# Feed-forward left sides formed during the output projection and parked in DRAM; residual steps tied to later pairs

## The chip, the core and the metric

One core of one Trainium2 chip runs the whole kernel as one program. The metric is device time in microseconds (us), the median over runs; lower is better. The kernel before took 1450.34 us (median of 3 runs, 1446.51 to 1451.52). The engines are named as on the profile page: PE is TensorE (matmuls), DVE is VectorE, ACT is ScalarE, POOL is GpSimd, and SP is SyncE, whose queue issues nearly all DMAs in program order.

## The reference, cut to what matters

The block normalises, projects, mixes attention with gated linear attention, and ends like this (1024 tokens, D = 1024, feed-forward width 4096, float32):

```
x  = layernorm(alpha * x + merged @ w_out)          # output projection, first layer norm: "x1"
ff = square(relu(x @ w_ff1 + b_ff1)) @ w_ff2 + b_ff2
x  = layernorm(alpha * x + ff)
```

## The kernel before, in words

**Precision.** Every float32 operand is split into a rounded high part and a low remainder: ACT casts the high part, DVE subtracts it from the operand for the low part (`split_to`, `halve`). A product is three matmuls per 128 rows of contraction: high by high (line 100), high by low of the moving side (line 101), low by high (line 102). A side is one such split operand of 128 x 512.

**Output projection** (lines 948 to 952 and the loop from 1018). The first 512 columns run in two halves of the contraction for all eight token tiles; the second 512 columns follow tile by tile. After each tile DVE adds the residual (line 930), takes the statistics (936, 941, 942) and normalises (976). PE then transposes the tile (`x1t`, line 997), ACT applies gain and bias (1000), and DVE forms differences of quarters (992), which are split into sides.

**First feed-forward matrix** (`pair1`). Two blocks of 128 hidden columns make a pair; there are 16 pairs. Each pair is a 2 x 2 by 2 x 2 block product done with seven products in place of eight (m1 to m7, each 12 matmuls). The weight's quarters A11, A12, A21, A22 give left sides A11, A12, A22, S1 = A21 + A22, S2 = S1 - A11, S3 = A11 - A21 and S4 = A12 - S2. The activations' quarters B11 to B22 give right sides T1 = B12 - B11, T2 = B22 - T1, T3 and T4. A pair's raw weight is loaded by two DMAs of 512 KB (line 1056); nine DVE operations on 128 x 512 (four sums or differences, five low parts) and five ACT casts make S1 to S4 and A22. A11 and A12 of pairs 0 and 1 are split earlier ("early", line 1029).

**The first two pairs** run side by side with the last transposes (lines 1194 to 1226): m1 and m2 of both, then m5, m3, m6, m7, m4. m5 needs T1, which needs the transposes of the last token tile.

**Residual.** x1 waits in DRAM (`x1dr`). For the second layer norm, sixteen pieces of 128 x 512 are loaded, multiplied by the gain (line 1247), given a bias (1248) and written back. The source hangs two of them on each of pairs 2 to 9; three broadcast vectors of 512 KB (line 1233) come first.

**What sets the order.** The source states the work; a scheduler with its own cost model then lays down each engine's instruction order at build time. At run time each engine, and SP's queue, goes through its list strictly in order. `issue_after` keeps the scheduler from putting an instruction ahead of a named one on the same engine; it adds no wait at run time. Sides live in a ring of seven buffers (`fraw`, `fwhi`, `fwlo`, `wc`), raw weights in a ring of five.

## Time and profile before

| what | value |
|---|---|
| median of 3 runs | 1450.34 us |
| the profiled execution | 1448.67 us, span 1446.9 us |
| PE busy | 1400.9 us, 97% of the span |
| DVE busy | 994.1 us, 69% |
| ACT busy | 622.4 us, 43% |
| DMA, mean | 158 GB/s, 227.98 MB in all |
| stretch 813.7 to 910.0 | 96.3 us, of which PE is busy 83.5, DVE 84.4 |

Times of rows are counted from the span's start. The stretch in the last line is where the first pairs of the feed-forward begin: it starts at the end of the products of "early". Before and after it PE is busy without a break.

### The profile page before, as it was taken

The numbers are of one execution on the slowest core, as the hardware profiler recorded it, in microseconds if no ns is written. First come the engines' busy times: TensorE is split into PE (matmuls) and PEld (weight loads), VectorE is DVE, ScalarE is ACT, GpSimd is POOL, SyncE is SP. The second block draws the span as 40 slices with busy tenths as digits, with TensorE's granted clock in tenths as the row PEclk, the third lists the DMA queues.
The fourth block names the chain that finished last, engine by engine and source line by source line (L and its number), as shares of the span: only waits on it lengthen the run. The fifth ranks groups of instructions, "written<-read, shape, count | busy, mean of one in ns | idle before, by whom it ended". The sixth has DMA issues, their size and how long they took to land.

```text
span 1446.9 us, 18910 instructions
## 1 busy us (share of the span) xinstructions
PE 1400.9 (97%) x6842; PEld 1167.8 (81%) x6842; DVE 994.1 (69%) x1710; ACT 622.4 (43%) x1180; POOL 84.6 (6%) x67
## 2 busy tenths in 40 slices
PE   8999889989999999999999898999999999999997
PEld 6989887877888888878888676888888888888885
DVE  5155745777555578566646988776666798786988
ACT  5244532434433344345405743555455633433333
POOL 2220312000000000022000000000000000000001
PEclk9999999999999999999999899999999999999999
DMA  7242403495543454275612476854433883544313
GB/s 232 70 132 63 153 31 123 153 280 180 178 144 128 137 165 136 82 231 167 242 58 87 146 243 240 302 170 154 156 139 116 287 331 117 189 131 145 100 47 117
DMA packets 122522, 227.98 MB, mean 158 GB/s; under 512 B 20685, under 2 KB 53709, under 8 KB 122428
## 3 DMA queue, kind: packets, MB, share of 16 engines
q1 hardware_dynamic: 122284, 226.57, 47.4%
q8 instruction: 54, 0.88, 0.3%
q14 instruction: 40, 0.33, 0.1%
q10 hardware_dynamic: 144, 0.20, 0.0%
HBM read 155.32 MB, written 72.44 MB: 157 GB/s over the span
## 4 chain that ended last, share of the span: by engine, by line
PE 86%; DVE 6%; DMA 5%; issue 1%; ACT 1%; SPq 0%; POOL 0%; DVEq 0%; ACTq 0%; POOLq 0%
PE ps L100 16%; PE ps L102 16%; PE ps L101 16%; PE mm L100 10%; PE mm L101 10%; PE mm L102 10%; PE avp L733 3%; DMA x1dr<-res 2%; PE sc L699 2%; PE tr L720 1%; DMA res<-x1dr 1%; PE sc L372 1%; DMA tb<-in_b_ff 1%; DVE T L982 0%; DVE xr L992 0%
## 5 line engine op out<-in xcount | busy, mean ns | idle before, releaser
L93 POOL TENSOR_TENSOR wlo<-raw,whi 128x768 fp32r<-128x768 f32 (+2 forms) x26 | 57.4, 2212 | 505.0 <-ACT whi L91 497.6
L981 ACT CAST T<-hp 128x1024 fp32r<-128x1024 f32 x36 | 37.9, 1052 | 110.0 <-PE ps L101 70.3
L100 PE MATMUL mm<-whi,x 128*128 128x272 f32 (+1 forms) x256 | 81.0, 317 | 0.0
L101 PE MATMUL mm<-wlo,x 128*128 128x272 f32 (+1 forms) x256 | 80.6, 315 | 0.0
L102 PE MATMUL mm<-whi,x 128*128 128x272 f32 (+1 forms) x256 | 80.5, 314 | 0.0
L101 PE MATMUL ps<-B,B 128*128 128x512 f32 x160 | 62.4, 390 | 0.0
L102 PE MATMUL ps<-B,B 128*128 128x512 f32 x160 | 62.3, 389 | 0.0
L100 PE MATMUL ps<-B,B 128*128 128x512 f32 x160 | 61.0, 391 | 0.5 <-ACT B L981 0.5
L100 PE MATMUL ps<-T,fraw 128*128 128x512 f32 x128 | 52.2, 409 | 7.6 <-ACT T L981 5.3
L102 PE MATMUL ps<-B,T 128*128 128x512 f32 x144 | 56.2, 390 | 0.0
L100 PE MATMUL ps<-B,T 128*128 128x512 f32 x144 | 56.2, 390 | 0.0
L102 PE MATMUL ps<-T,T 128*128 128x512 f32 x144 | 56.1, 390 | 0.0
L101 PE MATMUL ps<-T,T 128*128 128x512 f32 x144 | 56.0, 389 | 0.0
L100 PE MATMUL ps<-T,T 128*128 128x512 f32 x144 | 56.0, 389 | 0.0
L101 PE MATMUL ps<-B,T 128*128 128x512 f32 x144 | 56.0, 389 | 0.0
L1360 DVE TENSOR_TENSOR acc<-ps,acc 128x512 f32<-128x512 f32 x68 | 45.8, 689 | 12.9 <-PE ps L102 12.2
L982 DVE TENSOR_TENSOR T<-hp,T 128x1024 fp32r<-128x1024 f32 x36 | 44.0, 1223 | 15.3 <-ACT T L981 15.2
L100 PE MATMUL mm<-x,whi 128*128 128x512 f32 x120 | 47.6, 408 | 6.9 <-ACT x L146 5.8
L709 ACT ACTIVATE e<-e,sm 128x256 f32<-128x256 f32 (+2 forms) x96 | 43.2, 452 | 24.5 <-DVE sm L704 24.4
L101 PE MATMUL ps<-T,fraw 128*128 128x512 f32 x128 | 52.0, 406 | 1.2 <-DVE T L982 1.2
L102 PE MATMUL ps<-T,fraw 128*128 128x512 f32 x128 | 51.5, 404 | 0.0
L542 DVE TENSOR_TENSOR cr<-cu,mm 128x512 f32<-128x512 f32 x42 | 33.7, 805 | 23.2 <-PE mm L102 22.3
(424 smaller groups left out, 4166.5 us busy)
## 6 DMA issues: line engine op xcount, KB each, us to landing
hdr<-c SPq DMA_DIRECT2D x112, 256.0 KB, 2.5
hp<-hdr SPq DMA_DIRECT2D x56, 512.0 KB, 3.7
spill<-cr SPq DMA_DIRECT2D x56, 256.0 KB, 2.6
gate<-spill SPq DMA_DIRECT2D x32, 256.0 KB, 3.0
wa<-in_w SPq DMA_DIRECT2D x16, 512.0 KB, 5.0
wb<-in_w SPq DMA_DIRECT2D x16, 512.0 KB, 6.8
praw<-in_wfm SPq DMA_DIRECT2D x14, 512.0 KB, 4.2
pwhi<-in_wfm SPq DMA_DIRECT2D x14, 512.0 KB, 3.8
```

The costliest lines, as they stand in the source:

```text
L93: (lo_eng or G).tensor_tensor(lo, raw, hi.bitcast(F32), op=OP.subtract)
L100: T.matmul(ps, lh, rh, start=first and i == 0, stop=False, skip_group_check=more)
L101: T.matmul(ps, lh, rl, start=False, stop=False, skip_group_check=more)
L102: T.matmul(ps, ll, rh, start=False, stop=last and i == n - 1, skip_group_check=more)
L372: T.matmul(ap[d][:, i], kd[pr, cs], qd[pr, cs], start=True, stop=True)
L542: V.tensor_tensor(o, a, b, op=OP.add)
L699: T.matmul(sps[i][:, pr, 0:w], q[ps_, pr], k[ps_, pr, 0:w], start=True, stop=True)
L709: issued["exp"] = A.activation(e, e, AF.Exp, bias=sm[:, h:h + 1], scale=-1.0, accum_out=sm[:, 4 + h:5 + h])
L733: T.matmul(av[:, h * 64:h * 64 + 64], b["et"][h % 2][p0:p0 + vv.shape[0], h // 2, j], vv[:, h * 64:h * 64 + 64], start=j == 0, stop=j == n ...
L981: A.copy(o[:, 0], src)
L982: V.tensor_tensor(o[:, 1], src, o[:, 0].bitcast(F32), op=OP.subtract)
L1360: V.tensor_tensor(m, p, m, op=OP.add)
```

## The change

The pairs 0 and 1 no longer load their raw weight there and no longer form S1 to S4 and A22 there. A function `park` does this during the first half of the output projection, interleaved with its matmul calls: load, nine DVE operations and five casts for each pair, and each finished side (high and low, 512 KB) is written to a DRAM tile `sdr`. In the first pairs, `parked` then loads each side back into its ring buffer by one DMA. The raw loads of pairs 2 and 3 are issued a little earlier in the source. The residual's vectors and pieces move from pairs 2 to 9 to pairs 4 to 11, and are bound by `issue_after` to the latest raw weight load (loads) and to the add of m6 of their pair (arithmetic); the switch of the side memory to the second matrix moves from pair 12 to pair 13.

```diff
--- before.py
+++ after.py
@@ -107,6 +107,7 @@
...
     ygdr = dr.tile([4, 128, S], F32, name="ygdr")
+    sdr = dr.tile([2, 5, 128, 2, 512], F32, name="sdr")
     yadr = dr.tile([2, 128, S], F32, name="yadr")
...
@@ -946,9 +947,48 @@

     w += [wo_piece(wob, k2) for k2 in (2, 3)]
     ps = [bank8() for _ in range(8)]
-    for ks in (range(0, 4), range(4, 8)):
-        for t in range(8):
-            wout(t, 0, w, ps[t], ks)
+
+
+
+    sp_ = P.open("sides", reuse_waits="tile")
+    s_raw, s_out = ring(sp_, [128, 2, 512], F32, 2, "sraw"), ring(sp_, [128, 2, 512], F32R, 2, "sout")
+    s_sum = sp_.tile([128, 512], F32, name="ssum")
+
+    def park(j):
+        wr = {}
+
+        def keep(n, src):
+            o = s_out()
+            halve(o[:, 0], o[:, 1], src)
+            SP.dma_start(sdr[j, n], o.bitcast(F32))
+
+        def load():
+            for f in range(2):
+                t = s_raw()
+                SP.dma_start(t, io["w1"][2 * j + f].rearrange("p (h k) f -> p h (k f)", h=2))
+                wr[f] = t
+
+        def s1():
+            V.tensor_tensor(s_sum, wr[1][:, 0], wr[1][:, 1], op=OP.add)
+            keep(0, s_sum)
+
+        def s2():
+            V.tensor_tensor(s_sum, s_sum, wr[0][:, 0], op=OP.subtract)
+            keep(1, s_sum)
+
+        def s4():
+            V.tensor_tensor(s_sum, wr[0][:, 1], s_sum, op=OP.subtract)
+            keep(2, s_sum)
+
+        def s3():
+            V.tensor_tensor(wr[1][:, 0], wr[0][:, 0], wr[1][:, 0], op=OP.subtract)
+            keep(3, wr[1][:, 0])
+
+        return [load, s1, s2, s4, s3, lambda: keep(4, wr[1][:, 1])]
+
+    merge_streams([lambda t=t, ks=ks: wout(t, 0, w, ps[t], ks) for ks in (range(0, 4), range(4, 8)) for t in range(8)],
+                  park(0) + park(1))
+    P.close("sides")
     w = [load_w(io["wo"][1, k2], [128, 2, 512], V) for k2 in range(4)]
     P.close("wob")
     P.close("woa")
@@ -1053,7 +1093,7 @@
                 st["w"] = {}
                 for f in range(2):
                     w = f1_raw().bitcast(F32)
-                    SP.dma_start(w, io["w1"][2 * j + f].rearrange("p (h k) f -> p h (k f)", h=2))
+                    issued["load"] = SP.dma_start(w, io["w1"][2 * j + f].rearrange("p (h k) f -> p h (k f)", h=2))
                     for h in range(2):
                         st["w"][f, h] = w[:, h]
             return st["w"]
@@ -1064,22 +1104,34 @@
             c[nm] = cs[(7 * j + n if j > 1 else 4 * j + n if n < 4 else 4 + 3 * j + n) % 10]
             return c[nm]

+        def parked(nm, n):
+            st[nm] = o = f1_side().bitcast(F32R)
+            SP.dma_start(o.bitcast(F32), sdr[j, n])
+
         def s1():
+            if j < 2:
+                return parked("S1", 0)
             w = raw()
             st["s"] = f1_sum()
             V.tensor_tensor(st["s"], w[1, 0], w[1, 1], op=OP.add)
             st["S1"] = left(st["s"])

         def s3():
+            if j < 2:
+                return parked("S3", 3)
             w = raw()
             V.tensor_tensor(w[1, 0], w[0, 0], w[1, 0], op=OP.subtract)
             st["S3"] = left(w[1, 0])

         def s2():
+            if j < 2:
+                return parked("S2", 1)
             V.tensor_tensor(st["s"], st["s"], raw()[0, 0], op=OP.subtract)
             st["S2"] = left(st["s"])

         def s4():
+            if j < 2:
+                return parked("S4", 2)
             V.tensor_tensor(st["s"], raw()[0, 1], st["s"], op=OP.subtract)
             st["S4"] = left(st["s"])

@@ -1101,6 +1153,8 @@
             st["A12"] = early(1) if j < 2 else left(raw()[0, 1])

         def a22():
+            if j < 2:
+                return parked("A22", 4)
             st["A22"] = left(raw()[1, 1])

         def m1():
@@ -1117,7 +1171,7 @@

         def m6():
             mm("Y", st["S2"], "T2")
-            V.tensor_tensor(c["u2"], c["u2"], ps["Y"], op=OP.add)
+            issued["add"] = V.tensor_tensor(c["u2"], c["u2"], ps["Y"], op=OP.add)

         def m7():
             mm("W", st["S3"], "T3")
@@ -1183,8 +1237,6 @@
-    p0["raw"]()
-    p1["raw"]()
     SP.dma_start(x1dr[7], acc[7])
     def both(*names):
         for n in names:
@@ -1216,36 +1268,43 @@
     both("m5", "s2", "s4", "m3e")
     sums()
     both("s3")
+    pairs[2]["raw"]()
+    pairs[3]["raw"]()
     xsum("T2", x7, "x7", XR[1][:, 4:8])
     both("m6")
     xsum("T3", xp, "act", XR[1][:, 0:4])
     both("m7", "u3", "c22", "a22")
     xsum("T4", bp, "actb", XR[0][:, 4:8])
-    pairs[2]["raw"]()
-    pairs[3]["raw"]()
     both("h12", "m4", "h21")
     P.close("xraw")


-    resp = P.open("res", side="right", reuse_waits="tile")
-    ga, bb, tb = (resp.tile([128, D], F32, name=n) for n in ("ga", "bb", "tb"))
-    for n, v in (("ln1_g", ga), ("ln1_b", bb), ("b_ff2", tb)):
-        bvec(None, io[n], n, v)
-    V.tensor_scalar(ga, ga, ALPHA, None, op0=OP.mult)
-    V.scalar_tensor_tensor(bb, bb, ALPHA, tb, op0=OP.mult, op1=OP.add)
-    res_t = ring(resp, [128, 512], F32, 4, "res")
+    rs = {}
+
+    def res_open():
+        resp = P.open("res", side="right", reuse_waits="tile")
+        ga, bb, tb = (resp.tile([128, D], F32, name=n) for n in ("ga", "bb", "tb"))
+        with tc.issue_after(issued["load"].ins):
+            for n, v in (("ln1_g", ga), ("ln1_b", bb), ("b_ff2", tb)):
+                bvec(None, io[n], n, v)
+        V.tensor_scalar(ga, ga, ALPHA, None, op0=OP.mult)
+        V.scalar_tensor_tensor(bb, bb, ALPHA, tb, op0=OP.mult, op1=OP.add)
+        rs.update(t=ring(resp, [128, 512], F32, 4, "res"), ga=ga, bb=bb)

     def residual(i):
         t, h = i // 2, slice(i % 2 * 512, i % 2 * 512 + 512)
         r = {}

         def load():
-            r["t"] = res_t()
-            SP.dma_start(r["t"], x1dr[t, :, h])
+            r["t"] = rs["t"]()
+            with tc.issue_after(issued["load"].ins):
+                SP.dma_start(r["t"], x1dr[t, :, h])

         def do():
-            V.tensor_tensor(r["t"], r["t"], ga[:, h], op=OP.mult)
-            V.tensor_tensor(r["t"], r["t"], bb[:, h], op=OP.add)
+
+            with tc.issue_after(issued["add"].ins):
+                V.tensor_tensor(r["t"], r["t"], rs["ga"][:, h], op=OP.mult)
+                V.tensor_tensor(r["t"], r["t"], rs["bb"][:, h], op=OP.add)
             SP.dma_start(x1dr[t, :, h], r["t"])
         return load, [do]

@@ -1282,10 +1341,12 @@
     for j in range(2, NJ):
         st = list(pairs[j]["steps"])
         for i in (2, 5):
-            if j < 10:
-                load, do = residual(2 * j - 4 + (i > 2))
+            if 4 <= j < 12:
+                load, do = residual(2 * j - 8 + (i > 2))
                 st[i] = (lambda a=st[i][0], b=load: (a(), b())), st[i][1] + do
-        if j == 12:
+        if j == 3:
+            st[0] = st[0][0], [res_open] + st[0][1]
+        if j == 13:
             st[0] = st[0][0], [switch] + st[0][1]
         steps += st
     run(steps, 3)
```

The instruction lists show three places. In the changed kernel the lines shown have later numbers: 976 becomes 1016, 982 becomes 1022, 992 becomes 1032.

DVE, from the statistics of the last token tile (acc7) on, before. `xr0` and `xr1` are the transposed quarters; line 1070 is the sum of S1 and line 1075 the difference of S3, for pairs 0 and 1:

```order
L936 BN_STATS sts_6311<-acc7_5685 128x6
L1070 TENSOR_TENSOR c0_5928<-fwlo_6346 128x512
L941 BN_AGGR mv_6314<-sts_6311 128x2
L992 TENSOR_TENSOR xr0_5932<-xr1_5933,xr0_5932 128x4x128
L1075 TENSOR_TENSOR fwlo_6346<-fwlo_6345,fwlo_6346 128x512
L942 TENSOR_SCALAR mv_6314<-mv_6314 128x1
L992 TENSOR_TENSOR xr1_5933<-xr1_5933 128x4x128
L982 TENSOR_TENSOR B22_6263<-xr1_5933,B22_6263 128x4x128
L976 TENSOR_SCALAR acc7_5685<-acc7_5685,mv_6314 128x1024
L1070 TENSOR_TENSOR c0_5928<-fwhi_6342 128x512
L992 TENSOR_TENSOR xr1_5933<-xr1_5933,xr0_5932 128x4x128
L992 TENSOR_TENSOR xr0_5932<-xr1_5933,xr0_5932 128x4x128
```

The same place in the changed kernel:

```order
L937 BN_STATS sts_6363<-acc7_5686 128x6
L942 BN_AGGR mv_6366<-sts_6363 128x2
L943 TENSOR_SCALAR mv_6366<-mv_6366 128x1
L1032 TENSOR_TENSOR xr0_5984<-xr1_5985,xr0_5984 128x4x128
L1016 TENSOR_SCALAR acc7_5686<-acc7_5686,mv_6366 128x1024
L1032 TENSOR_TENSOR xr1_5985<-xr1_5985 128x4x128
L1022 TENSOR_TENSOR B22_6315<-xr1_5985,B22_6315 128x4x128
L1032 TENSOR_TENSOR xr1_5985<-xr1_5985,xr0_5984 128x4x128
L1032 TENSOR_TENSOR xr0_5984<-xr0_5984,xr1_5985 128x4x128
L1032 TENSOR_TENSOR xr0_5984<-xr1_5985,xr0_5984 128x4x128
L1032 TENSOR_TENSOR xr1_5985<-xr1_5985 128x4x128
L1022 TENSOR_TENSOR T1_6439<-xr0_5984,T1_6439 128x384 x4
```

The three operations of pairs 0 and 1 are gone from these rows, and the first pieces of T1 (line 1022, `T1`), which stood 18 rows behind the statistics, stand 11 behind them. On PE, the eight transposes of acc7 stand 12 matmuls earlier than before; the rest of PE's list up to there is the same.

DVE during the first half of the output projection, before: the last parts of the first half's weight (`wo`), the low parts of the second half's weight (`wlo`), then the first evacuation (line 930):

```order
L147 TENSOR_TENSOR wo12_5690<-raw_5687,wo02_5689 128x1024
L147 TENSOR_TENSOR wo13_5696<-raw_5693,wo03_5695 128x1024
L93 TENSOR_TENSOR wlo_5903<-raw_5899,whi_5901 128x1024
L93 TENSOR_TENSOR wlo_5909<-raw_5905,whi_5907 128x1024
L93 TENSOR_TENSOR wlo_5915<-raw_5911,whi_5913 128x1024
L93 TENSOR_TENSOR wlo_5921<-raw_5917,whi_5919 128x1024
L930 SCALAR_TENSOR_TENSOR acc0_5671<-acc0_5671,ps0_5118 128x512
L936 BN_STATS sts_5961<-acc0_5671 128x6
```

The same place in the changed kernel; `sraw`, `ssum` and `sout` belong to `park` of pair 0:

```order
L148 TENSOR_TENSOR wo12_5691<-raw_5688,wo02_5690 128x1024
L148 TENSOR_TENSOR wo13_5697<-raw_5694,wo03_5696 128x1024
L972 TENSOR_TENSOR ssum_5707<-sraw1_5704 128x512
L984 TENSOR_TENSOR sraw1_5704<-sraw0_5703,sraw1_5704 128x512
L148 TENSOR_TENSOR sout0_5705<-ssum_5707,sout0_5705 128x512
L976 TENSOR_TENSOR ssum_5707<-ssum_5707,sraw0_5703 128x512
L93 TENSOR_TENSOR wlo_5955<-raw_5951,whi_5953 128x1024
L93 TENSOR_TENSOR wlo_5961<-raw_5957,whi_5959 128x1024
L148 TENSOR_TENSOR sout1_5706<-ssum_5707,sout1_5706 128x512
L980 TENSOR_TENSOR ssum_5707<-sraw0_5703,ssum_5707 128x512
L148 TENSOR_TENSOR sout0_5705<-ssum_5707,sout0_5705 128x512
L93 TENSOR_TENSOR wlo_5967<-raw_5963,whi_5965 128x1024
```

Pair 0's operations stand before and between the `wlo` parts; pair 1's stand further down, between the evacuations.

SP's queue, where the residual's vectors and first pieces are loaded, before:

```order
L919 DMA ga_6711<-in_ln1_g 128x1024
L919 DMA bb_6712<-in_ln1_b 128x1024
L1056 DMA fwhi_6342<-in_w1 128x1024
L919 DMA tb_6713<-in_b_ff2 128x1024
L1244 DMA res0_6719<-x1dr_87 128x512
L1244 DMA res1_6720<-x1dr_87 128x512
L1244 DMA res2_6721<-x1dr_87 128x512
L1244 DMA res3_6722<-x1dr_87 128x512
L1056 DMA fwlo_6346<-in_w1 128x1024
L1056 DMA w14_6463<-in_w1 128x1024
L1249 DMA x1dr_87<-res0_6719 128x512
```

In the changed kernel, the second two residual loads and the first writes that follow them:

```order
L1301 DMA res2_6893<-x1dr_88 128x512
L1301 DMA res3_6894<-x1dr_88 128x512
L1144 DMA hdr_87<-c0_5980 128x512
L1144 DMA hdr_87<-c9_6516 128x512
L1144 DMA hdr_87<-c5_6512 128x512
L1144 DMA hdr_87<-c0_5980 128x512
L1144 DMA hdr_87<-c6_6513 128x512
L1308 DMA x1dr_88<-res0_6891 128x512
L1308 DMA x1dr_88<-res1_6892 128x512
```

Before, the residual stands directly behind the raw loads of the first pairs, and a piece's buffer is reloaded as soon as it is written. Now two pieces are loaded per pair, and the loads of one pair stand ahead of the writes of the pair before it.

## Rows read from the trace of the kernel before

**Rows 1.** Busy time by stretch: engine busy (x instructions), clock, DMA share, GB/s
```profile
696.00:752.00 56.00, 56.00 (x246) 45.78 (x245) 31.47 (x43) 13.87 (x19) 0.00 (x0) 1.00 0.45 158
813.70:846.00 32.30, 25.74 (x97) 19.79 (x96) 28.84 (x48) 17.91 (x35) 0.00 (x0) 0.84 0.46 162
846.00:866.00 20.00, 19.02 (x82) 15.34 (x83) 18.30 (x31) 10.67 (x18) 0.00 (x0) 1.00 0.65 217
866.00:880.00 14.00, 10.41 (x38) 7.82 (x37) 13.17 (x23) 5.42 (x9) 0.00 (x0) 0.88 0.78 277
880.00:910.00 30.00, 28.32 (x123) 22.68 (x123) 24.08 (x40) 12.06 (x22) 0.00 (x0) 1.00 0.74 252
910.00:950.00 40.00, 40.00 (x176) 32.60 (x175) 28.35 (x46) 22.05 (x38) 0.00 (x0) 1.00 0.74 265
1200.00:1300.00 100.00, 99.50 (x438) 81.90 (x438) 81.49 (x90) 35.16 (x36) 0.00 (x0) 1.00 0.49 153
```

**Rows 2.** Who TensorE waited for, 800 to 960: us in total, times, longest
```profile
PE ps L100 <- DVE c L1126: 1.8, 1, 1.8
PE ps L100 <- ACT fwlo L981: 1.8, 1, 1.8
```

**Rows 3.** Timeline of TensorE: start, duration, [idle before <- releaser]
```profile
803.57 1.04 PE L997 MATMUL ps<-ident,acc 128*128 128x128 f32 x8
...
810.03 1.04 PE L997 MATMUL ps<-ident,acc 128*128 128x128 f32 x8
...
813.47 0.40 PE L102 MATMUL ps<-B,early 128*128 128x512 f32 x1
819.16 1.22 PE L100 MATMUL ps<-T,fraw 128*128 128x512 f32 x2 [5.30 <-ACT T L981]
...
822.18 0.79 PE L101 MATMUL ps<-T,fraw 128*128 128x512 f32 x1 [1.18 <-DVE T L982]
...
826.61 0.53 PE L102 MATMUL ps<-T,fraw 128*128 128x512 f32 x1
...
850.00 0.47 PE L100 MATMUL ps<-B,fwhi 128*128 128x512 f32 x1 [0.58 <-DVE c L1147]
```

**Rows 4.** Timeline of VectorE, 800 to 822
```profile
800.97 0.69 DVE L936 BATCH_NORM_STATS2 sts<-acc 128x6 f32<-128x512 f32 x1
803.65 0.69 DVE L1070 TENSOR_TENSOR c<-fwlo 128x512 f32<-128x512 f32 x1 [1.99 <-DMA fwlo<-in_w]
...
806.80 0.81 DVE L976 TENSOR_SCALAR acc<-acc,mv 128x1024 f32<-128x1024 f32 x1
...
811.13 1.29 DVE L982 TENSOR_TENSOR fraw<-c,fraw 128x512 fp32r<-128x512 f32 x2
...
821.43 0.70 DVE L982 TENSOR_TENSOR T<-xr,T 128x512 fp32r<-128x512 f32 x1
```

**Rows 5.** Timeline of ScalarE, 808 to 819
```profile
808.24 1.15 ACT L981 CAST fraw<-c 128x512 fp32r<-128x512 f32 x2 [0.86 <-DVE c L1070]
...
810.29 1.77 ACT L981 CAST T<-xr 128x384 fp32r<-128x384 f32 x4
...
812.53 2.90 ACT L1000 ACTIVATE xr<-ps,cols 128x128 f32<-128x128 f32 x8
...
818.43 0.68 ACT L981 CAST T<-xr 128x512 fp32r<-128x512 f32 x1
```

**Rows 6.** Line 1247: duration ns min/median/max, first and last start
```profile
L1247 DVE TENSOR_TENSOR res<-res,ga x16: 685/693/700, 845.0 to 898.2; 128x512 f32<-128x512 f32 x16
```

**Rows 7.** Who VectorE waited for, 842 to 906
```profile
DVE res L1247 <- DMA res<-x1dr: 8.4, 9, 2.2
```

**Rows 8.** DMA issues, 690 to 910: count, KB each, median us to landing
```profile
fwlo<-in_w SPq DMA_DIRECT2D x6, 512.0 KB, 5.0
```

**Rows 9.** The low parts wlo, 700 to 760: duration ns, first and last start
```profile
L101 PE MATMUL ps<-wlo,mg x13: 395/396/397, 751.5 to 759.9; 128*128 128x512 f32 x13
...
L93 DVE TENSOR_TENSOR wlo<-raw,whi x4: 1225/1226/1227, 722.4 to 730.9; 128x1024 fp32r<-128x1024 f32 x4
```

## The prediction

> **What bounds the kernel now.** I read the page first: PE is busy 97% of the span, so only stretches where PE idles, or runs at half clock, can give time back. The second view is busy time by stretch [rows 1] (columns after the stretch: its length, then PE, weight loads, DVE, ACT, POOL). From 910 to 950 PE is never idle and does 176 matmuls in 40 us, 0.2273 us each. I use that as the full rate and ask of each stretch what its matmuls would need:
>
> - 813.7 to 846: 97 matmuls need 22.05 of 32.3 us; lost 10.25 (idle 6.56, the rest at a granted clock of 0.84).
> - 846 to 866: 82 need 18.64 of 20; lost 1.36.
> - 866 to 880: 38 need 8.64 of 14; lost 5.36 (clock 0.88).
> - 880 to 910: 123 need 27.96 of 30; lost 2.04.
>
> Together 19.0 us. That is the most this change can win, since PE loses next to nothing before and after.
>
> Third, why. The timeline of PE [rows 3] shows the first loss: after the last product of "early" (813.47) PE idles until 819.16 for the ACT cast of the last piece of T1, then until 822.18 for DVE's low part of it. The 11 matmuls from 822.18 to 826.61 come every 0.44 us instead of 0.23: PE is at the lower of its two levels (1.2 GHz) after the long idle. The timeline of DVE [rows 4] shows what T1 waited behind. The statistics of token tile 7 end at 801.66; then DVE stands 1.99 us for a raw weight of pair 0, and until T1's low part ends at 822.13 it does 12 operations of pairs 0 and 1 (the four sums and differences S1 and S3, the two S2, five low parts, and S4 of pair 0), 0.60 us each when back to back (two in 1.29). ACT has five casts of the same sides in between [rows 5]. The later losses are mainly two waits of 1.8 us for DVE and ACT [rows 2], in a stretch where DVE is busy 94% (866 to 880) and holds the residual: 16 pieces from 845.0 to about 903 [rows 6], two operations each, 32 x 0.60 = 19.2 us, with another 8.4 us of standing for residual loads [rows 7].
>
> **Part 1: S1 to S4 and A22 of pairs 0 and 1 are loaded ready.** Removed from DVE between 803 and about 842: 18 operations x 0.60 = 10.8 us, and the 1.99 us of standing; from ACT ten casts of about 0.52 (two in 1.15, [rows 5]). What is late next? I follow T1 in the changed order. Tile 7's transposes stand 12 matmuls earlier on PE: 810.03 - 12 x 0.233 = 807.2 [rows 3], done at 808.0. DVE is ready for that: without the raw wait and two operations between 801.66 and 806.80, tile 7 is normalised by about 804.4. ACT then sets the pace [rows 5]: tile 6's evacuation of 2.90 us from 804.6, when its transposes end (803.57 + 1.04), a copy to 808.0, T1's four casts of 1.77 to 809.8, one more cast to 810.3, tile 7's evacuation of 2.90 to 813.2, a relu to 813.8, the last cast of T1 to 814.4 (before: 819.1; copy and relu are taken like a cast, 0.5 to 0.6). DVE's low part follows by 815.1 (before: 822.13). So of the 6.56 us idle at the head, about 1.0 us stays, in two gaps of 0.7 and 0.3.
>
> Does the clock fall at these gaps? A wait of 0.58 us before 850.00 [rows 3] lies in a stretch granted 1.00; the waits of 1.8 and 1.8 lie in one granted 0.88 [rows 1, 2]. The new gaps are nearest to the first, so I take no loss; the other end is the 11 slow matmuls of before, 11 x 0.21 = 2.3 us. The Trainium skill ("TensorE: Matmul & The Clock Gate", Part 1: The HAM clock gate) says that half rate is the default and that only recent activity releases the full clock. By that rule any new pause is a risk, and with the clock lost at the head the sum would be 2.3 us worse; the 0.58 us row speaks against it for so short a pause.
>
> After the head PE has m5, m3, m6 and m7 of both pairs, 96 matmuls, 21.8 us without a break if their sides are there. T2, T3 and T4 need twelve more DVE pieces, 7.2 us, so DVE is done by about 825, when m6 begins. The sides come by DMA. The ring buffers of S2 and S4 come free with the last matmuls of the output projection, at about 799.9; their four loads are first in SP's queue there, then x1 and four raw loads of pairs 2 and 3. At 5.0 us to landing [rows 8], and eight transfers of 0.5 MB at the 252 GB/s of the 880 to 910 row, the fourth lands by 808 and the eighth by 817; m3 needs S4 at 815. S3 and A22 reuse buffers that m5 and m6 free at 818 to 828, and are needed from 831. Cost taken: 0. The upper bound is one late load, 5.0 us.
>
> **Part 2: the same work during the output projection.** Added to 707 to 752: 18 DVE operations (10.8 us), ten casts (5.2 us), four loads and ten writes of 0.5 MB. From 696 to 752 DVE is busy 31.5 of 56 us and ACT 13.9 [rows 1], so there is room for both. The order matters more: pair 0's operations stand ahead of the low parts of the second weight half, which were done at 732.1 and which PE first uses at 751.5 [rows 9]. On DVE seven operations, 4.2 us, stand before or between them; on SP the raw loads of that half stand behind one write of a side. Even two loads and a write in series (15 us at 5.0 each) stay within the 19 us of slack. Cost 0. Pair 1's operations stand between evacuations of banks that PE takes up again only 20 us later, so a DVE that stands 5 us for its reload costs nothing either.
>
> **Part 3: the residual.** It leaves the stretch 843 to 903 and comes back as four DVE operations, 2.4 us, in each of pairs 4 to 11. A pair is 84 matmuls, 19.1 us. DVE was busy 71% of 910 to 950, and 2.4 of 19.1 adds 13%: 84%. The nearest row is 1200 to 1300, DVE 81% busy, where PE does 438 matmuls in 100 us and loses 0.45 us. Over eight pairs, 153 us, that is 0.7 us. The other end is what 846 to 910 lost with the same 32 operations in it: 1.36 + 5.36 + 2.04 = 8.8 us. I take the first, because DVE no longer stands for loads: in SP's new order the loads of one pair go out ahead of the writes of the pair before, and before they went out behind the write that freed the buffer. The vectors (line 1233) can still hold DVE once around pair 4; for this and for small waits like the one of 0.58 at 850.00 I put 1.0 us, an estimate.
>
> **Sum.** -19.0 + 1.0 + 0.7 + 1.0 = -16.3 us, against the profiled execution's 1448.67: 1432.4. The median of before is 1.67 above that execution, so the median forecast is 1434.
>
> **Rivals.**
> A. The residual costs the same wherever it stands. DVE runs in order, so four more operations behind m6's add hold up the next evacuation and the next side. For it: the waits of 1.8 us [rows 2]. Against: eight pairs instead of three. Then 8.8 stays: -19.0 + 1.0 + 8.8 + 1.0 = -8.2, 1442; with the clock also lost at the head, 1444.5.
> B. The parked sides arrive late. 14 transfers of 0.5 MB are added to one queue, and S3 and A22 wait there behind stores. For it: 5.0 us per load. Against: the slack above. Each product that waits costs up to 5.0 and some half clock: with two, 1444.
> C. The change doesn't do what it says: T1 was only the first of several waits. ACT sits a step behind DVE, and m6 and m7 wait for T2 and T3 instead, with the residual again in the way in pairs 4 and 5. Gain under 4 us: 1448.
> D. Slower. Every pair from 4 to 11 meets a wait and half clock, as 866 to 880 did (5.36 us). The place is m7's evacuation behind the two residual multiplications. Eight times 5.36 is 43 us against the 17 won: 1476. It decides from 2.1 us per pair. For it: DVE stood for residual loads nine times, up to 2.2 us [rows 7]. Against: the loads now go out a pair ahead.
>
> **How the numbers follow.** Forecast 0.58 (1430 to 1438), A 0.20, B 0.07, C 0.09, D 0.06. About 0.3%, 4.4 us, is what a measurement of this kernel can tell from no change. Forecast, A and B end below 1446: faster 0.85; C is the same, 0.09; slower 0.06. The range 1429 to 1446 takes in all 19 us won at one end, and A with the clock lost and a late load at the other.
>
> **What would show it.** T1's low part ends at about 815 and PE starts the bulk of m5 within 2 us of the end of "early", with the clock at 1.00 from 813 to 846; 97 matmuls of that stretch take 23 to 24 us; the stretch that followed, to pair 4, has no PE wait over 1 us; 696 to 800 has none either, with DVE about 11 us busier; and residual operations lie from about 860 to 1030, two loads a pair, without PE waits beside them. The prediction is wrong if PE waits for `sdr` loads, if the second weight half is late at 752, or if PE loses over 2 us per pair in pairs 4 to 11.

## The result and the profile after

The changed kernel took 1435.28 us (median of 4 runs, 1432.0 to 1435.46) against 1448.65 for the kernel before on the same chip (four runs, of which the 1450.34 at the head is the median of the first three): a ratio of 0.990, 95% interval 0.988 to 0.992. The forecast was 1434. The profiled execution took 1435.09 us (before: 1448.67), so 13.6 us less, where the sum had said 16.3.

The busy time by stretch comes first, engine by engine as in [rows 1]. Three stretches of 32, 64 and 140 us are counted from the end of the last product that reads "early", because everything behind that point starts from it. Before:

```profile
813.87:845.87 32.00, 25.53 (x96) 19.79 (x96) 28.54 (x48) 17.61 (x35) 0.00 (x0) 0.84 0.47 163
845.87:909.87 64.00, 57.68 (x240) 45.75 (x240) 55.54 (x92) 28.14 (x48) 0.00 (x0) 0.97 0.72 246
909.87:1049.87 140.00, 140.00 (x612) 114.55 (x611) 97.22 (x154) 74.32 (x122) 0.00 (x0) 1.00 0.54 189
```

and after, in the same view, with the stretch of the parked work first:

```profile
696.00:752.00 56.00, 56.00 (x246) 45.86 (x245) 38.00 (x54) 20.06 (x29) 0.00 (x0) 1.00 0.72 261
816.94:848.94 32.00, 31.73 (x138) 25.82 (x139) 23.94 (x39) 18.08 (x33) 0.00 (x0) 1.00 0.39 134
848.94:912.94 64.00, 64.00 (x281) 52.43 (x280) 46.50 (x74) 32.38 (x54) 0.00 (x0) 1.00 0.61 206
912.94:1052.94 140.00, 139.06 (x604) 112.75 (x604) 109.22 (x176) 69.33 (x116) 0.00 (x0) 1.00 0.62 223
```

Read the number behind PE's busy time, the matmuls done. At the full rate of about 0.228 us each, the first 32 us win 42 matmuls (9.6 us), the next 64 us win 41 (9.3), and the 140 us in which the residual now stands lose 8 (1.8). The list of PE's waits from 690 to 1110 us is now short (columns as in [rows 2]; u3, line 1180, is the add behind m7); the waits of 5.3, 1.8 and 1.8 of before are gone:

```profile
PE ps L100 <- DVE c L1180: 0.9, 3, 0.5
PE ps L100 <- ACT T L1021: 0.3, 1, 0.3
```

The timelines at the head answer to [rows 3 to 5]. The last product of "early" starts at 816.54; ACT ends its last cast of T1 0.6 us later, and DVE's low part (817.19) follows at once. TensorE:

```profile
816.54 0.40 PE L102 MATMUL ps<-B,early 128*128 128x512 f32 x1
817.21 0.73 PE L100 MATMUL ps<-T,fraw 128*128 128x512 f32 x2 [0.27 <-ACT T L1021]
```

ScalarE and VectorE:

```profile
813.17 2.90 ACT L1040 ACTIVATE xr<-ps,cols 128x128 f32<-128x128 f32 x8
815.92 0.73 ACT L1140 ACTIVATE c<-ps,cols 128x512 f32<-128x512 f32 x1
816.49 0.66 ACT L1021 CAST T<-xr 128x512 fp32r<-128x512 f32 x1
```
```profile
817.19 0.69 DVE L1022 TENSOR_TENSOR T<-xr,T 128x512 fp32r<-128x512 f32 x1 [0.40 <-ACT T L1021]
```

**Where the missing 3 us are.** "early" ends at 816.94 after and at 813.87 before, 3.07 us later, although up to the output projection the instructions stand in the same order on every engine. From that point to the end of the span it is 616.36 us after and 633.03 before: 16.7 us less, against 16.3 forecast. Matched one by one in order, the same matmul starts 0.62 us later after than before from 20 to 120 us, 2.16 us later at 140 and 3.07 us later from 650 on. All of the delay stands ahead of the first load of parked work (711.9), so the moved work did not cause it. Half of it arises between 120 and 140 us. From 115 to 130, before and after:

```profile
115.00:130.00 15.00, 13.83 (x95) 12.51 (x94) 6.68 (x11) 9.11 (x26) 2.44 (x4) 1.00 0.25 67
```
```profile
115.00:130.00 15.00, 13.83 (x85) 12.51 (x84) 5.00 (x9) 9.22 (x26) 2.44 (x4) 0.89 0.25 67
```

PE is idle for the same 1.17 us, yet in one execution the granted clock stays at 1.00 and in the other it falls to 0.89, which costs ten matmuls in this stretch. Of the 12 profiled executions of this study six show 1.00 (94 or 95 matmuls) and six 0.89 (85). A cast on ACT that comes right behind starts at 148.9 to 149.7 in the first six and at 150.5 to 151.4 in the others. The changed kernel's profile fell on one side and before's on the other. The other half of the delay comes in small steps that were not followed up. So below each kernel's time from the end of "early" to the end of its span is given beside its median: it leaves this difference out.

### The profile page after: what moved, and what is told of

It reads as the page before. It is cut to its first block, busy times and chain, and to the rows that moved or that the text cites. A ratio compares the mean times of both kernels' runs of the same rounds, so it can differ in the third digit from the quotient of the medians.

```text
span 1433.3 us, 18978 instructions
## 1 busy us (share of the span) xinstructions
PE 1398.6 (98%) x6842; PEld 1167.5 (81%) x6842; DVE 995.3 (69%) x1710; ACT 621.1 (43%) x1180; POOL 84.5 (6%) x67
## 4 chain that ended last, share of the span: by engine, by line
PE 85%; DVE 7%; DMA 4%; ACT 2%; issue 2%; SPq 0%; POOL 0%; DVEq 0%; ACTq 0%; POOLq 0%
PE ps L100 15%; PE ps L101 15%; PE ps L102 15%; PE mm L100 10%; PE mm L101 10%; PE mm L102 10%; PE avp L734 3%; PE sc L700 2%; PE tr L721 1%; DMA fwhi<-in_w 1%; DMA w<-in_w 1%; PE sc L373 1%; PE av L383 0%; DMA xr<-in_xT 0%; PE sc L344 0%
## 5 line engine op out<-in xcount | busy, mean ns | idle before, releaser
L1140 ACT ACTIVATE c<-c,cols 128x512 f32<-128x512 f32 x48 | 34.7, 725 | 47.9 <-DVE c L1186 32.4
L100 PE MATMUL ps<-T,fraw 128*128 128x512 f32 x128 | 50.6, 397 | 1.2 <-DVE c L1180 0.9
L101 PE MATMUL ps<-T,fraw 128*128 128x512 f32 x128 | 50.1, 392 | 0.0
```

The costliest lines, as they stand in the source:

```text
L100: T.matmul(ps, lh, rh, start=first and i == 0, stop=False, skip_group_check=more)
L101: T.matmul(ps, lh, rl, start=False, stop=False, skip_group_check=more)
L1140: A.activation(q, src, AF.Relu, bias=cols[:, 2 * j + f:2 * j + f + 1])
```

## The experiments

Each kernel ran on one chip beside the kernel before. "From early" is the time in the profiled execution from the end of the last product of "early" to the end of the span; the last column has the matmuls done in the 32, the next 64 and the next 140 us.

| kernel | median us | before, same chip | ratio, 95% interval | from early | matmuls 32 / 64 / 140 |
|---|---|---|---|---|---|
| before | 1448.65 | | | 633.0 | 96 / 240 / 612 |
| the change | 1435.28 | 1448.65 | 0.990 (0.988 to 0.992) | 616.4 | 138 / 281 / 604 |
| the change again | 1430.38 | 1449.21 | 0.987 (0.986 to 0.989) | 615.2 | 138 / 281 / 608 |
| sides only | 1444.83 | 1450.45 | 0.996 (0.995 to 0.997) | 627.8 | 130 / 230 / 612 |
| residual only | 1441.16 | 1450.45 | 0.993 (0.992 to 0.994) | 623.4 | 97 / 280 / 613 |
| tied, pairs 2 to 9 | 1433.17 | 1450.45 | 0.988 (0.987 to 0.990) | 616.9 | 138 / 280 / 603 |
| no residual arithmetic | 1431.06 | 1450.45 | 0.986 (0.985 to 0.988) | 614.2 | 139 / 281 / 613 |
| residual arithmetic twice | 1430.48 | 1450.47 | 0.986 (0.984 to 0.987) | 614.4 | 139 / 281 / 612 |
| parked work twice | 1452.88 | 1450.47 | 1.002 (1.001 to 1.003) | 615.4 | 139 / 281 / 607 |
| order only | 1437.21 | 1450.47 | 0.990 (0.989 to 0.992) | 620.9 | 108 / 280 / 613 |
| tied behind u3 | 1430.14 | 1450.47 | 0.986 (0.984 to 0.988) | 614.3 | 138 / 281 / 613 |
| pair 0 parked, u3 | 1438.33 | 1449.21 | 0.992 (0.991 to 0.993) | 620.4 | 113 / 279 / 612 |

**1. The sides alone.** The residual goes back to pairs 2 to 9, opened ahead of the loop, without ties:

```diff
-            with tc.issue_after(issued["load"].ins):
-                SP.dma_start(r["t"], x1dr[t, :, h])
+            SP.dma_start(r["t"], x1dr[t, :, h])
...
-            if 4 <= j < 12:
-                load, do = residual(2 * j - 8 + (i > 2))
+            if j < 10:
+                load, do = residual(2 * j - 4 + (i > 2))
```

(the same for the multiplications and the vectors).

> The left sides of pairs 0 and 1 are parked as in the changed kernel; the residual stands in pairs 2 to 9 as before, without the two ties. In the order of instructions its 32 operations on DVE then lie in one cluster, right behind the splits of T4. Theory (head and residual are two separate losses): the head is as in the changed kernel (loss after the end of 'early' about 1 us), and about 8.8 us of waits and half clock stay beside the residual; time 1448.7 - 10.25 + 1 = about 1439 to 1440, and PE waits of 1 to 3 us for DVE and ACT within 40 us of the first residual operation. Rival 1 (the residual hurt only because DVE was already late from the sides): PE does not wait beside the residual either, time 1435 as with the whole change. Rival 2 (the residual was the main thing): 1446.

It won 5.2 us from "early" on, less than the 9.3 expected, and no rival fits. For T1 PE waits only 0.3 us, as in the full change. But the cluster of residual operations now starts 20 us behind the end of "early" (833.0) instead of 31 [rows 6] and costs more than it did before: 130 matmuls in 32 us, where the full change has 138, and 230 in 64 us, where before had 240. Busy time by stretch, and two of PE's waits:

```profile
812.90:844.90 32.00, 30.42 (x130) 24.27 (x131) 24.85 (x40) 14.20 (x26) 0.00 (x0) 1.00 0.59 200
844.90:908.90 64.00, 55.00 (x230) 43.48 (x229) 50.71 (x84) 27.93 (x47) 0.00 (x0) 0.95 0.83 291
```
```profile
PE ps L100 <- ACT c L1140: 6.5, 1, 6.5
PE ps L100 <- ACT c L1164: 1.6, 1, 1.6
```

ACT, which PE waits for, itself stands behind DVE, and DVE is never idle there for long: from 850 to 869 its residual operations stand between the steps of the products. So the two parts are not independent. With the residual left where it was, 11.6 us (51 matmuls) are lost behind the head, and the sides' gain is partly eaten. The ties alone decide where the residual stands: built with the residual in pairs 4 to 11 but without the ties, the program has the same instructions in the same order as this kernel, on every engine. The place in the source moved nothing.

**2. The residual alone.** Before, with the residual and its ties as in the change.

> The kernel before with the residual alone moved and tied to pairs 4 to 11; all left sides are formed at the head as before. Theory: the head keeps its loss of about 10 us (PE idle 5 to 6 us for T1, granted clock near 0.84 in the 30 us behind it), and the stretch behind it loses 1 to 2 us instead of 8.8; time 1448.7 - 8.8 + 1.7 = about 1441 to 1442. Rival (the waits behind the head come from the sides' delay, and the residual only fills gaps): the waits stay, time 1447. With the sides alone and this run the two gains should add up to the gain of the whole change, about 13 to 16 us.

It won 9.6 us from "early" on (expected: 7 to 8). Stretches and the whole list of PE's waits from "early" to 1060:

```profile
815.99:847.99 32.00, 25.19 (x97) 19.85 (x98) 29.06 (x49) 18.59 (x37) 0.00 (x0) 0.84 0.27 83
847.99:911.99 64.00, 64.00 (x280) 52.33 (x280) 49.78 (x80) 35.99 (x59) 0.00 (x0) 1.00 0.61 214
911.99:1051.99 140.00, 140.00 (x613) 114.64 (x612) 108.01 (x173) 73.15 (x117) 0.00 (x0) 1.00 0.62 219
```
```profile
PE ps L100 <- ACT T L981: 5.6, 1, 5.6
PE ps L101 <- DVE T L982: 1.2, 1, 1.2
```

The head keeps its whole loss, and the 64 us behind it lose nothing at all: the waits there came from the residual, not from the delayed sides. The rival (1447) is out. The two gains add up to 14.9 us, against 16.7 and 17.8 for two executions of the whole change.

**3. Two pairs earlier.** The ties kept, the residual in pairs 2 to 9.

> The changed kernel with the residual in pairs 2 to 9 instead of 4 to 11, its ties kept (each load behind the raw loads of its pair, each multiplication behind the add of m6). Theory A (the tie, that is four operations per pair instead of a cluster, is what saves): time within 1.5 us of the changed kernel, 1435 to 1437. Theory B (pairs 2 and 3 stand beside the tail of pairs 0 and 1, where DVE has no room): PE waits of over 1 us in pairs 2 and 3, about half of the 8.8 us comes back, 1439.

Theory A holds: 616.9 from "early", within 0.6 us of the change. Its loss sits in one wait of 1.9 us for the add u3, at 980 us, in neither pair 2 nor pair 3.

**4. Without the residual's arithmetic.** The two multiply and add operations are left out, so the residual lacks its scale and bias.

> The changed kernel with the two operations per piece of the residual left out (32 on DVE; the loads and the write-backs stay), so that its output lacks the scale and bias of the first LayerNorm in the residual. Theory: in pairs 4 to 11 the residual costs PE 0.7 us, so the time falls by 0.5 to 1 us, to about 1434.5, which is inside the noise. Rival A (the residual costs the same wherever it stands, 8.8 us): 1427.

From "early" it is 614.2: the residual costs the change 2.1 us (1.0 in its second execution), not 0.7 and not 8.8. Rival A is out by size, and the small price is 1.4 to 3 times the term in the sum. The median alone does not show it, since its spread is 4 us.

**5. Twice the residual's arithmetic.**

```diff
             with tc.issue_after(issued["add"].ins):
+                V.tensor_tensor(r["t"], r["t"], rs["bb"][:, h], op=OP.add)
+                V.tensor_tensor(r["t"], r["t"], rs["bb"][:, h], op=OP.subtract)
                 V.tensor_tensor(r["t"], r["t"], rs["ga"][:, h], op=OP.mult)
```

> The changed kernel with two more DVE operations per piece of the residual (an addition and a subtraction of the bias ahead of the two that are there; the result is the same up to rounding): 8 instead of 4 per pair in pairs 4 to 11, that is 2.4 us more of DVE in 19.1 us, about 91% busy where the changed kernel shows 78%. Theory (DVE's share is what matters, and there is room up to about 90%): PE loses 0.3 to 1 us more per pair, time 1437 to 1443. Rival D of the prediction (a pair with residual in it meets a wait and half clock as soon as DVE is late): 5.36 us per pair, 43 us, about 1478.

Both were wrong. PE loses nothing in the 140 us, with DVE 90% busy, where the change loses 0.94 us idle at 78%:

```profile
911.34:1051.34 140.00, 140.00 (x612) 114.67 (x612) 125.94 (x207) 70.99 (x116) 0.00 (x0) 1.00 0.60 212
```

So it is not DVE's share that sets the price. The added operations also changed the order: in every pair exactly two residual operations stand between the add of m6 and u3, where the change has two in three pairs, three in two and four in three. The next run asks whether what stands ahead of u3 is the price.

**6. Tied behind u3.** In the change, residual operations stand between the add of m6 (line 1174) and u3, whose bank PE needs next. VectorE and TensorE of the change in one of the first pairs that hold the residual, from the first operation on the pair's raw weight (line 1116) on:

```profile
933.09 0.69 DVE L1116 TENSOR_TENSOR c<-fwlo 128x512 f32<-128x512 f32 x1 [2.76 <-DMA fwlo<-in_w]
...
935.03 0.68 DVE L1174 TENSOR_TENSOR c<-c,ps 128x512 f32<-128x512 f32 x1
935.63 1.29 DVE L1306 TENSOR_TENSOR res<-res,ga 128x512 f32<-128x512 f32 x2
...
938.64 0.68 DVE L1307 TENSOR_TENSOR res<-res,bb 128x512 f32<-128x512 f32 x1
939.24 0.68 DVE L1180 TENSOR_TENSOR c<-c,ps 128x512 f32<-128x512 f32 x1
```
```profile
939.98 0.50 PE L100 MATMUL ps<-T,fraw 128*128 128x512 f32 x1 [0.51 <-DVE c L1180]
```

The edit moves the tie:

```diff
-            issued["add"] = V.tensor_tensor(c["u2"], c["u2"], ps["Y"], op=OP.add)
+            V.tensor_tensor(c["u2"], c["u2"], ps["Y"], op=OP.add)
...
-            V.tensor_tensor(ct("h22"), c["u2"], ps["W"], op=OP.add)
+            issued["add"] = V.tensor_tensor(ct("h22"), c["u2"], ps["W"], op=OP.add)
```

> The changed kernel with the two residual multiplications tied behind the add after m7 (u3) instead of the one after m6. In the changed kernel PE waits three times (0.9 us in all) for just this add, behind residual operations, and from the end of 'early' plus 96 us it does 604 matmuls in 140 us where the kernel without residual arithmetic does 613. Theory (those three pauses are the whole price of the residual): they go, PE does 610 to 613 matmuls there, and the time from the end of 'early' to the end falls by 1.5 to 2 us. Rival: the next add (c22 or h21) is late instead, and nothing is won.

As the theory said: 613 matmuls in the 140 us, no wait, 614.3 from "early", the same as without any residual arithmetic. DVE now does u3 first:

```profile
932.97 0.68 DVE L1180 TENSOR_TENSOR c<-c,ps 128x512 f32<-128x512 f32 x1
933.56 1.29 DVE L1306 TENSOR_TENSOR res<-res,ga 128x512 f32<-128x512 f32 x2
```

This is the best of the versions with one residual (1430.14). By medians it cannot be told from the change.

The place of the tie is only one half of that price. The kernel of experiment 2 keeps the change's tie, and in each pair all four residual operations stand ahead of u3 (there line 1126), yet PE does 613 matmuls in the 140 us and waits for nothing:

```profile
936.60 0.69 DVE L1120 TENSOR_TENSOR c<-c,ps 128x512 f32<-128x512 f32 x1 [0.53 <-PE ps L102]
937.20 1.29 DVE L1254 TENSOR_TENSOR res<-res,ga 128x512 f32<-128x512 f32 x2
...
939.01 1.28 DVE L1255 TENSOR_TENSOR res<-res,bb 128x512 f32<-128x512 f32 x2
...
942.02 0.68 DVE L1126 TENSOR_TENSOR c<-c,ps 128x512 f32<-128x512 f32 x1
```

There DVE comes to the add of m6 ahead of PE in six of the eight pairs and waits for it. In the change DVE comes to that add without a wait, behind PE, and in each pair it stands for the raw weight shortly before: 20.1 us in the 140, against 8.2 in experiment 2 and 6.5 in experiment 5. PE's three pauses, and the wait of 1.9 us in experiment 3, each come in a pair whose raw weight DVE had stood 2.8 to 4.2 us for. The later tie took the price away with 16.2 us of such waits still there. So the price shows only where both come together, a late raw weight and residual operations ahead of u3. That is read from these waits and not tested by itself: no run changed the raw weights alone, and why DVE stands longer for them in the change stays open.

**7. The change again.**

> The changed kernel a second time, unaltered, to see on the same chip and beside the other run what differs between two executions. From the end of 'early' to the end 616.0 to 616.8 us as before (616.36), since the order of its instructions is fixed there; the time up to the end of 'early', where nothing was changed before the output projection, may differ by 4 us between executions (812.8 to 816.9 in the runs so far). Rival: the part behind 'early' differs by 2 us as well, and the 2 us won by the later tie of the residual are noise.

The theory's band was missed: 615.2, not 616.0 to 616.8. The three pauses beside the residual are nearly absent (PE idle 0.07 us, 608 matmuls), so they depend on when things arrive in an execution. Of the 2.1 us that the later tie won over the first execution, 0.9 remain over the second; about half of the rival's 2 us is thus a difference between executions. What remains agrees with the matmuls: the kernel of experiment 10, whose residual has the same ties, does 607 in the 140 us and takes 615.4 us from "early"; those of experiments 4, 5 and 6 do 612 or 613 and take 614.2 to 614.4. Up to the end of "early" the two executions agree (816.94 and 816.87), both with the clock at 0.89 near 115 us.

**8. Is parking needed, or only the order?** Experiment 2 with S1 of both pairs moved behind T1:

```diff
-    with tc.issue_after(issued["pow"].ins):
-        both("s1")
     sums = x1t(7)
+    with tc.issue_after(issued["low"].ins):
+        both("s1")
```

("low" is the last low part of T1.)

> Nothing parked: the kernel of the residual move alone, with S1 of both pairs tied behind the last low part of T1, so that none of the sides stands before T1 on DVE. Theory (it is the amount of DVE work between the last statistics and the products that counts, not its order): T1 is ready at about 815, but then PE waits for S1 of pair 0, whose low part now stands eight operations behind T1; the head's loss stays at 5 us or more, time 1438 to 1442 (residual move alone: 1441). Rival (order was all that was wrong at the head): the loss at the head falls below 2 us, time 1434 to 1436, as with parking.

T1 is ready in time, and PE waits for S1 in its place. The median, 1437.21, lies between the theory's 1438 to 1442 and the rival's 1434 to 1436. The head decides: its 32 us lose 31 matmuls against 139 (7.1 us), over the theory's 5 us, so the rival is out. VectorE, with the low part of T1 at 814.85 and that of S1 at 821.48, and TensorE:

```profile
814.85 0.69 DVE L982 TENSOR_TENSOR T<-xr,T 128x512 fp32r<-128x512 f32 x1 [0.40 <-ACT T L981]
815.46 0.69 DVE L1070 TENSOR_TENSOR c<-fwhi 128x512 f32<-128x512 f32 x1
...
821.48 0.69 DVE L982 TENSOR_TENSOR fraw<-c,fraw 128x512 fp32r<-128x512 f32 x1
```
```profile
819.59 0.79 PE L100 MATMUL ps<-T,fraw 128*128 128x512 f32 x1 [5.00 <-ACT fraw L981]
```

Order alone wins 2.5 us over experiment 2 (620.9 against 623.4); parking on top of it, with the same 613 matmuls in the 140 us (the kernel tied behind u3), wins another 6.6 (614.3). The work has to leave the head, and its order is the smaller part.

**9. Only pair 0 parked** (tie behind u3).

> Only pair 0's left sides are parked, pair 1's are formed at the head as before; the residual is tied behind u3. In the order of instructions eight operations of pair 1's sides stand ahead of T1's last low part on DVE, where the kernel before has twelve and the changed kernel none. Theory (head loss goes with the number of DVE operations ahead of T1, and there is slack of a few operations behind ACT): PE idles 2 to 4 us for T1, half of the head's loss, 1433 to 1434. Rival 1 (the first operations are hidden behind tile 7's statistics and ACT): under 1 us, 1430 to 1431 as with both pairs parked. Rival 2 (the wait for a raw load and not the count is what delays T1): 5 us and half clock, 1438.

PE idles 3.7 us, inside the theory's 2 to 4, though not for T1: it waits for the last piece of B22, whose cast on ACT ends at 819.81, just ahead of T1's. The time is that of rival 2 (1438): the granted clock of the 32 us falls to 0.89, and 25 matmuls (5.7 us) are lost against 138. DVE also stands 1.92 us for a raw load until 805.83, much as before (1.99). Whether it is the number of operations or the late load that delays the head was not separated, here or in experiment 8, which takes both from ahead of T1. Parking half of the work left most of the head's loss.

**10. The parked work done twice.**

```diff
-                  park(0) + park(1))
+                  park(0) + park(1) + park(0) + park(1))
```

> The changed kernel with the parked work done twice over (both pairs formed and written a second time during the first half of the output projection): another 18 DVE operations, ten casts, four loads and ten writes. Theory (slack of 15 us or more stands before PE): the last low part of the second weight half moves from 737 to 744 to 750, PE takes it up at 754 without a wait, time within 1.5 us of the changed kernel (1435). Rival (the cover is nearly used up by the first copy): PE waits for the second weight half or for a bank, 5 us or more, 1440 and over.

A clear miss: the whole gain was lost. The second weight half was on time (its last low part at 737.5, as in the change), so the place that I had named as the limit is not the limit. Instead PE stood idle inside the output projection, for 16 of the 20 us from 786 to 806. Stretches, and then the first evacuation of tile 0 on ACT:

```profile
766.00:786.00 20.00, 19.96 (x99) 16.21 (x97) 16.14 (x28) 5.53 (x8) 1.64 (x3) 1.00 0.76 271
786.00:806.00 20.00, 3.80 (x13) 2.60 (x12) 9.91 (x19) 5.42 (x13) 1.08 (x2) 0.57 0.60 229
```
```profile
803.05 6.03 ACT L1040 ACTIVATE xr<-ps,cols 128x128 f32<-128x128 f32 x17 [3.48 <-DMA sdr<-sout]
```

ACT waits for the last side to be written to DRAM, since the evacuated tiles take the memory of the sides' buffers; PE's banks are not emptied, and PE stops. PE's own waits from 690 to 838 name this, and the normalisations that DVE did late among the extra sides. How the loss divides between the two was not separated:

```profile
PE ps L1037 <- DVE acc L1016: 8.5, 2, 5.3
PE ps L100 <- ACT xr L1040: 7.7, 1, 7.7
```

In the change the same evacuation starts at 771.8, and the last of its ten side writes is issued at 759.0 and lands some 2.6 us later. The slack of the parked work there is about 10 us; here the third pair's last low part came at 778.5, already beyond it.

## Why the prediction was right, and which steps were not

- **The bound and the losses.** All 19.0 us lay where the sum put them. Against the kernel before, 42 and 41 matmuls came back there, 18.9 us.
- **The head (19.0, of which 1.0 stays).** Right in mechanism and size. The forecast had ACT finish T1 0.9 us, and DVE 1.6 us, after the last product of "early" starts; measured 0.6 and 1.3. Of two gaps, 0.7 and 0.3, one of 0.27 came. ACT set the pace as worked out: evacuation, relu, last cast. Experiments 2, 8 and 9 show that it was the sides' work ahead of T1: with it in place PE waits 5.6 us, with half of it 3.7 (there for B22), without it 0.3; put behind T1 on the same engine it costs 5.0 us of waiting for S1. The clock stayed at 1.00 at the short gap, and was 0.84 to 0.89 in the 32 us behind the head in the four kernels with waits of 3.7 us and more there.
- **Parked loads (0).** No PE wait for any of them. One was slower than taken, 10.2 us to landing against 5.0, and hidden. Two lines of the issues from 795 to 815, columns as in [rows 8]:

```profile
fwhi<-sdr SPq DMA_DIRECT2D x2, 512.0 KB, 5.6
wc<-sdr SPq DMA_DIRECT2D x1, 512.0 KB, 10.2
```

- **Part 2 (0 by cover).** The zero was right: 56.00 of 56.00 us busy from 696 to 752, with DVE 6.5 us and ACT 6.2 busier than in [rows 1]. The reason was incomplete. I measured the cover at the second weight half, whose last low part now starts at 737.0 and ends at 738.2, and which PE takes up at 754.6, 16.4 us later. The tighter cover is not in the prediction: about 10 us from the landing of the last side to the first evacuation that reuses the sides' memory; experiment 10 found it. The low parts of that half were done at 732.1 before and came 6.1 us later, 3.07 of them from the execution's own delay, so 3.0 from the parked work, where seven operations, 4.2 us in all, had been counted.

```profile
L93 DVE TENSOR_TENSOR wlo<-raw,whi x4: 1216/1221/1226, 727.7 to 737.0; 128x1024 fp32r<-128x1024 f32 x4
L101 PE MATMUL ps<-wlo,mg x15: 395/396/397, 754.6 to 764.4; 128*128 128x512 f32 x15
```

- **The residual (8.8 removed, 0.7 added).** That the ties spread it over pairs 4 to 11 and that rival A and D fail is shown by experiments 1 to 5. The term 0.7 was mis-sized: 2.1 and 1.0 us in two executions. The step that failed is pricing it by DVE's share: 78% busy lost 2.1 us and 90% lost none. The price was pauses behind one add, at the place that rival D had named (m7's evacuation) and at a twentieth of its 43 us; the later tie removed it. The reason given, that DVE no longer stands for loads, held for the residual's own loads (none, against 8.4 us) and not for the raw weights (experiment 6). The operations ran from 896.9, later than the 860 forecast:

```profile
L1306 DVE TENSOR_TENSOR res<-res,ga x16: 684/686/687, 896.9 to 1032.6; 128x512 f32<-128x512 f32 x16
```

- **Vectors and small waits (1.0).** The cost was nothing: PE is busy 64.00 of 64.00 us behind the head. DVE does stand 1.9 us for one of the vectors; PE does not see it.
- **The total.** The terms left over were forecast at 2.7 us. Taking the 32 us as 139 matmuls, the head lost 0.2 and the residual 2.1, so 2.3. That is why 16.3 and 16.7 agree, and it is partly luck: the head and the small waits cost 1.8 us less than forecast and the residual 1.4 more. That the median came within 1.3 us of the forecast is luck too, since the same kernel's second median was 1430.38. The parts do not simply add up: the sides alone won 5.2 us of the 9.3 put down to them, the residual alone 9.6 against 7 to 8, together 14.9 where the whole change won 16.7 and 17.8.
- **The clock's rule.** I had weighed that any new pause might cost half clock. Where PE idled 1.17 us in pauses of at most 0.6 us, the clock fell in six executions of twelve; at the single new gap of 0.27 in none that had it; nor did it fall at the pauses behind u3, up to 1.9 us long (experiment 3). So the risk was real, but not at this place.

## What to carry to other kernels

Work that only depends on weights can be moved out of the stretch where the data-dependent chain is tight, through DRAM if need be; check not only who needs its result but who needs its buffers next. To spread filler work over later steps, tie it behind the very operation that frees what the bottleneck waits for: a place in the source may move nothing, and an engine's busy share does not tell the price. Whether that operation is late at all depends on what the engine had to wait for just before. Compare executions from a landmark behind which the programs differ, since what comes before it can vary by more than the effect.

## What the hardware showed that I had not expected

- With the same order of instructions and the same 1.17 us of idle time in 15 us, the granted clock from 115 to 130 us was 1.00 in six executions and 0.89 in six, and the work behind it stood about 2 us later in the latter. The Trainium skill ("TensorE: Matmul & The Clock Gate", Part 1: The HAM clock gate) says of the start of a kernel that the number of slow matmuls varies between runs of the same kernel; these rows agree, and show it in mid-kernel.
- With DVE busy 90% of 140 us, PE lost nothing (612 matmuls against 613 without any residual arithmetic).
- A load of 512 KB from the parked sides, issued at 807.5, took 10.2 us to land beside the raw loads of pairs 2 and 3, four of which took a median of 11.1; of the four parked loads issued from 798.9 to 801.2, two took a median of 5.3 and two of 5.6. From 800 to 813.7 the DMA engines were 95% busy and moved 359 GB/s.
